# Second mixer's output projection: four couples of seven products in its middle columns, sum tiles placed elsewhere, and two couples' token sums made one chunk ahead

## The chip, the cores and the metric

The kernel runs on one core of one Trainium2 chip. The time is the device time of a whole execution in microseconds (us). The kernel before was run three times, and each comparison uses the median of its runs. One execution more was taken with the hardware profiler; all rows of a profile below come from such an execution. The engines are TensorE (PE in the profile, with PEld for its weight loads), VectorE (DVE), ScalarE (ACT), GpSimd (POOL) and SyncE (SP), which issues nearly all of the transfers from memory.

## The reference

A two-layer encoder trunk on one sequence of 256 tokens with 2048 channels, in float32. Layer 0 mixes tokens with a bidirectional mLSTM, layer 1 with a bidirectional HGRN2; after each mixer comes a ConvGLU.

```python
for layer in range(DEPTH):
    hn = rmsnorm(h, norm_mix_g[layer])
    if layer % N_MIXERS == 0:
        mix = mlstm_mixer(hn, mlstm_w_in[j], ..., mlstm_w_out[j])
    else:
        mix = hgrn_mixer(hn, hgrn_w_in[j], ..., hgrn_w_out[j])
    h = h + mix
    h = h + conv_glu(rmsnorm(h, norm_ffn_g[layer]), ...)
return rmsnorm(h, final_g)
```

The change is in the last step of each mixer, and for the second mixer alone: `y = head_rmsnorm(y, ...) * jax.nn.silu(g)` and then `y @ w_out`, a product of 256 x 2048 with 2048 x 2048 that is added to `h`.

## The kernel before

**Products.** TensorE multiplies float32 weights and activations as pairs of two rounded parts: a high part and the rest. For a weight tile `raw`, ACT makes `wh` (line 146, a copy that rounds) and DVE makes `wl = raw - wh` (line 147). Each product is three matmuls, high by high, high by low, low by high (line 235 in the stage of interest). An activation tile (`yb` in the second mixer, 128 channels by 256 tokens, high and low side by side) is made at lines 377 and 378 from a transposed head, `pz` (transposed on PE at line 1123).

**Chunks and pieces.** The program is a list of chunks. A chunk of kind "tm" makes 512 output columns, and the chunks of a projection run in the order of the list `[c0, two, c3]`: `c0` has columns 0 to 511, `two` has the middle columns 512 to 1535, `c3` the rest. Weights arrive as `raw` tiles of 128 x 2048 (1 MB, three buffers, issued on SP at line 134) and are cut into pieces of 1024 columns; the generator `split_weights` keeps the conversions three pieces ahead of their use in program order. Small jobs (`side`) are pushed as generators and advance with each product.

**The pair.** The chunk `two` is of kind "st" and is handled by `squares_by_seven`. Its unit is a couple: two blocks of 128 input channels, 16 blocks or eight couples (0 to 7) in all. A plain couple multiplies a 2 x 2 block of activations (two token halves by two channel blocks) by a 2 x 2 block of weights (two channel blocks by two groups of 512 columns) with eight products, 24 matmuls. A couple in the list `seven` does it with seven products, 21 matmuls, as in Strassen's and Winograd's scheme. For that it needs sums of weights (T1 to T4) and of tokens (S1 to S4), and four more accumulators (`mm`, beside `pc` for the four results). PE takes the pieces of a couple in this order: for a plain one first B11 and B22, then B21 and B12; for one of seven products B11 and B22, then T2 and T3, then B21 and T1, then T4.

**Where the sums come from.** Weight sums: `combine` (line 206) makes them from a raw tile when it is there, by four DVE subtractions of 128 x 512, into a tile `T` and in place in `raw`. For a stored couple, `prepare` made them in an earlier stage (line 630, in tiles `praw` of the mixer's own pool) and wrote them to a scratch in memory, `tscr`; the pair then loads `T` (line 197) and a quarter of `raw` (line 198) from there. The first mixer combines on the fly, the second has its couples 2, 4 and 6 stored. Token sums: `token` adds the two token halves of each block into a tile `f` (line 671), and `token_sums` makes four differences of 128 x 128 in it (line 565), the high part `sx` on ACT (line 566) and the low part on DVE (line 567).

**Memory and time.** The tiles `T` and `f` have two buffers each in the pool "op". In the function `mixed` that pool is opened when chunk `c0` is done, at the place of the mixer's own pool ("hg" in the second mixer), which is closed there. So the first loads and sums in "op" wait for the last readers of the old pool. `c0`'s results are added to `hm` at line 548.

**Order.** The program is written in one order, and a scheduler then sets the order in which each engine is given its instructions. The order rows below show it.

Of the kernel before, what the change touches and what calls it, by code (L numbers as in the profile page):

```python
# [8 lines left out]
F32 = mybir.dt.float32  # L9
F32R = mybir.dt.float32r  # L10
I32 = mybir.dt.int32
AF = mybir.ActivationFunctionType
ALU = mybir.AluOpType
PSUM = bass.MemoryType.PSUM

P = 128
T = 256
D = 2048
KT = D // P
# [30 lines left out]
SEVEN = (2, 3, 4, 5, 6, 7, 8, 9), (1, 2, 3, 4, 5, 6, 7)  # L50
# [1 line left out]
SPLIT = (0, 2, 5), (0, 2, 5)  # L52
END = 3
SCRATCH = 4096
SEVEN_MIX = (2, 4, 6)

QUAD = 32
TMS = (0, 4, 8, 11, 15, 18, 21)
# [6 lines left out]
def trunk_kernel(ctx, tc, xT, x_d, fg_d, pp_d, cst_d, w_gate, w_first, w_aq, w_ak, w_av, w_ao, w_aout, w_ao2,  # L65
                 w_bq, w_bv, w_bg, w_bout, w_bo2, w_up, w_d0, w_d1, w_d3, out, mscr, tscr):
    nc = tc.nc
    act, dve, pool, pe = nc.scalar, nc.vector, nc.gpsimd, nc.tensor

    keep = ctx.enter_context(tc.tile_pool(name="keep", bufs=1))  # L70
# [49 lines left out]
    side, held = Side(), []  # L120
# [61 lines left out]
    def temporary(pool_, name):  # L182
        ff = pool_.name == "ff"
        return pool_.tile([P, 1536], F32, tag="avc" if ff else name, bufs=TEMP if ff else 2, name=name)
# [207 lines left out]
    def late(dst, src):  # L392
        tc.keep_in_program_order(nc.sync.dma_start(dst, src))
# [162 lines left out]
        return where.tile([P, 2 * T], F32R, tag=f"yt{j}", name=f"{name}{j}")  # L556


    def token_sums(mp, i, a, b, S, last=None):

        m = 384 if last else 512
        sx = mp.tile([P, 2 * m], F32R, tag=f"sx{i}", name="sx")
        for i, (x, y, op) in enumerate(((a[:, P:T], b[:, P:T], ALU.add), (a[:, P:T], a[:, 0:P], ALU.subtract),
                                        (S[:, 0:P], a[:, 0:P], ALU.subtract), (b[:, 0:P], S[:, 2 * P:3 * P], ALU.subtract))):
            dve.tensor_tensor(S[:, i * P:(i + 1) * P], x, y, op)
        act.copy(sx[:, 0:m], S[:, 0:m])
        dve.tensor_tensor(sx[:, m:2 * m], S[:, 0:m], sx[:, 0:m].bitcast(F32), ALU.subtract)
        if last:
            act.copy(last[0], S[:, m:512])
            dve.tensor_tensor(last[1], S[:, m:512], last[0].bitcast(F32), ALU.subtract)  # L570
        return [(sx[:, i * P:(i + 1) * P], sx[:, m + i * P:m + (i + 1) * P]) for i in range(m // P)] + ([last] if last else [])

    def pair(src, nk, c0, x, sums, norm, seven):

        def part(t, c):
            o = 512 * (c0 + c)
            return hm[:, t, o:o + 512]

        def mid(ps):
            P1, P6, P7, P5 = ps  # L580
            u = ev.tile([P, 512], F32, tag="jk", bufs=1, name="u")
            act.copy(u, P1)
            dve.tensor_tensor(part(0, 0), part(0, 0), P1, ALU.add)
            dve.tensor_tensor(u, u, P6, ALU.add)
            dve.tensor_tensor(part(0, 1), part(0, 1), P5, ALU.add)
            dve.tensor_tensor(part(0, 1), part(0, 1), u, ALU.add)
            dve.tensor_tensor(part(1, 1), part(1, 1), P5, ALU.add)
            dve.tensor_tensor(u, u, P7, ALU.add)  # L588
            pool.tensor_tensor(part(1, 0), part(1, 0), u, ALU.add)  # L589
            pool.tensor_tensor(part(1, 1), part(1, 1), u, ALU.add)  # L590

        def done(ps):
            for c in range(2):
                for t in range(2):
                    h = part(t, c)
                    dve.tensor_tensor(h, h, ps[2 * t + c], ALU.add)
                if norm is not None and c == 0:
                    norm.add(c0)
            if norm is not None:
                side.push(second())  # L600

        def second():
            yield 3.0
            norm.add(c0 + 1)

        ch = Chunk("st", src, nk, x, done)
        ch.mid, ch.seven, ch.sums = mid, seven, sums
        ch.stored, ch.waits, ch.pool, ch.ends, ch.rest = {}, (), None, False, False
        return ch
# [29 lines left out]
    early = ([], []), ([], [])  # L639

    def prepare_early(mp, layer, first, period):
        todo, finished = early[layer]
        side.push(prepare(lambda i: [mp.tile([P, 1024], F32, tag=f"p{j}", name="praw") for j in range(2)],
                          todo, first, period, finished, late, False))

    def store(ch, src, u, todo):
        ch.stored[u] = tscr[turns["t"]]
        turns["t"] += 1
        todo.append((src[:, 2048 * u:2048 * (u + 1)], ch.stored[u]))

    def mixed(w, w2, x, norm, close, layer=None):

        c0, _, _, c3 = project(lambda c: w[c // 3], KT, x, norm)
        op, SX, first = ExitStack(), {}, c0.done

        def sums(u):
            side.until(lambda: u in SX)
            return SX[u]

        two = pair(w2, KT, 1, x, sums, norm, SEVEN_MIX)  # L660
        if layer is not None:
            for u in SEVEN_MIX:
                store(two, w2, u, early[layer][0])
            two.waits = [early[layer][1]]

        def token():
            for i, u in enumerate(SEVEN_MIX):
                f = temporary(two.pool, "f")
                for j in range(2):
                    y = x(2 * u + j).bitcast(F32)  # L670
                    dve.tensor_tensor(f[:, j * T:(j + 1) * T], y[:, 0:T], y[:, T:2 * T], ALU.add)
                SX[u] = token_sums(two.pool, i, f[:, 0:T], f[:, T:2 * T], f[:, 2 * T:4 * T])
                yield 5.0

        def done(ps):
            side.drain()
            close()
            two.pool = op.enter_context(tc.tile_pool(name="op", bufs=1))
            two.pool.tile([P, LEAD], F32, name="lead")
            first(ps)  # L680
            side.push(token())

        c0.done, c3.before = done, op.close
        return [c0, two, c3]


# [278 lines left out]
    def hgrn(norm, nxt):  # L965
        YT = [None] * KT
        stack = ExitStack()
        box = {}

        def begin():  # L970
            mp = box["mp"] = stack.enter_context(tc.tile_pool(name="hg", bufs=1))
            late(cst[:, C_LV:], cst_d[:, C_LV:])
            prepare_early(mp, 1, 30.0, 38.0)
            box["turn"] = 0
            lb = box["lb"] = mp.tile([P, KT], F32, name="lb")
            oml = box["oml"] = mp.tile([P, KT], F32, name="oml")
            t0 = mp.tile([P, 2, KT], F32, name="t0")
            t1 = mp.tile([P, KT], F32, name="t1")
            raw = pp[:, OFF["lb"]:OFF["lb"] + 2 * KT].rearrange("p (a b) -> p a b", a=2)
            dve.tensor_tensor(t1, raw[:, 0], raw[:, 1], ALU.max)  # L980
            for i in range(2):
                dve.tensor_tensor(t0[:, i], raw[:, i], t1, ALU.subtract)
            act.activation(t0, t0, AF.Exp)
            dve.tensor_tensor(t1, t0[:, 0], t0[:, 1], ALU.add)
            dve.reciprocal(t1, t1)
            for i in range(2):
                dve.tensor_tensor(t0[:, i], t0[:, i], t1, ALU.mult)
            dve.tensor_tensor(lb, t0[:, 0], t0[:, 1], ALU.add)
            dve.tensor_tensor(lb, lb, t0[:, 0], ALU.subtract)
            dve.tensor_scalar(oml, lb, -1.0, 1.0, ALU.mult, ALU.add)  # L990

        def blocks(z, h):
            return bass.AP(z.tensor, z.offset, [list(z.ap[0]), [640, 2], [2 * h, T // (2 * h)], [T + h, 2], [1, h]])
# [134 lines left out]
        chunks, vs, gs, fs = [], [], [], []  # L1128
# [26 lines left out]
        for n, ch in enumerate(fs):  # L1155
            if n in TMS:
                i = TMS.index(n)
# [4 lines left out]
        def yx(k):  # L1162
            side.until(lambda: YT[k] is not None)
            return YT[k]

        return chunks + mixed(w_bout, w_bo2, yx, nxt, stack.close, 1)


    def ffn(layer, norm, nxt):
# [91 lines left out]
    chunks = mlstm(n0, n1)  # L1261
# [3 lines left out]
    b = c[0].before  # L1265
# [85 lines left out]
def build(nc, ins, out_shape=(2, P, D), **kw):  # L1351
    ap = {k: nc.dram_tensor("in_" + k, a.shape, mybir.dt.from_np(a.dtype), kind="ExternalInput").ap()
          for k, a in ins.items()}
    out = nc.dram_tensor("out", out_shape, F32, kind="ExternalOutput").ap()
    mscr = nc.dram_tensor("mscr", (64, T), F32, kind="Internal").ap()
    tscr = nc.dram_tensor("tscr", (len(SEVEN_MIX) + 4 * len(SEVEN[0]) + 4 * len(SEVEN[1]), P, 2048), F32, kind="Internal").ap()
    with tile.TileContext(nc, schedule_with_timeline_sim=True) as tc:  # L1357
        with ExitStack() as ctx:
            trunk_kernel(ctx, tc, ap["xT"], ap["x"], ap["fg"], ap["pp"], ap["cst"], ap["w_gate"], ap["w_first"],
                         ap["w_aq"], ap["w_ak"], ap["w_av"],  # L1360
                         ap["w_ao"], ap["w_aout"], ap["w_ao2"], ap["w_bq"], ap["w_bv"], ap["w_bg"],
                         ap["w_bout"], ap["w_bo2"], ap["w_up"], ap["w_d0"], ap["w_d1"], ap["w_d3"], out, mscr, tscr, **kw)
# [12 lines left out]
```

## Time and profile before

| | |
|---|---|
| median of three runs | 2370.63 us (2369.7 to 2372.42) |
| the profiled execution | 2372.48 us, of which 2370.5 are the profile's span |
| PE busy | 2358.8 us, 14563 matmuls |
| DVE busy | 1968.9 us |
| ACT busy | 1464.2 us |
| POOL busy | 197.8 us |
| the pair of the second mixer | from about 1608 us of the span |
| TensorE's granted clock, mean | 0.999 |

A row of a timeline gives the start (us from the span's start), the length, the engine, the line, the operation, the tile written and the tiles read, their shape and type and how many such instructions follow each other; in brackets the idle time of the engine ahead of it and what ended that. On one engine the length of an instruction and the start of the next overlap a little, so the distance from start to start says what one costs. In a table of windows each engine has its busy time and, in brackets, the instructions begun.

### The profile page before, as it was taken

Reading aid. Unit: us, or ns where it says so; the run is one execution under the profiler, and the core shown is the slowest. Engines: PE = TensorE matmul, PEld = TensorE weight load, DVE = VectorE, ACT = ScalarE, POOL = GpSimd, SP = SyncE. Lnnn points to the kernel's source line nnn. Section 1 sums busy time; section 2 is a strip of 40 time slices with the busy share of each in tenths; the row PEclk is TensorE's granted clock in tenths of the full one; section 3 lists DMA queues with packets and bytes.
Section 4 is the critical chain, followed back from the end, with each engine's and each line's share of the span. In section 5 each row is a group of like instructions: output and inputs, shape, how many; then the busy total and the mean of one; then the engine's idle time right before and its main releaser. Section 6 shows DMA issues by size and latency. Waiting matters only on the chain. (4 is left out here: it accounts for less than half of the span.)

```text
span 2370.5 us, 38366 instructions
## 1 busy us (share of the span) xinstructions
PE 2358.8 (100%) x14563; PEld 2019.7 (85%) x14563; DVE 1968.9 (83%) x3033; ACT 1464.2 (62%) x2322; POOL 197.8 (8%) x244
## 2 busy tenths in 40 slices
PE   9999999999999999999999999999999999999998
PEld 8888888888888888888888888888888888888887
DVE  7777687889888898887887888778788888888888
ACT  7655456555565555665777777676555566555565
POOL 0100000000000000000232322220000000000000
PEclk9999999999999999999999999999999999999999
DMA  8776656888888888986556665546788898888896
GB/s 303 237 246 243 213 195 212 296 283 290 320 314 321 306 284 289 358 303 228 211 203 212 216 218 209 208 172 230 266 301 283 292 339 313 292 295 298 313 346 221
DMA packets 122120, 632.96 MB, mean 267 GB/s; under 512 B 13760, under 2 KB 14784, under 8 KB 77520
## 3 DMA queue, kind: packets, MB, share of 16 engines
q1 hardware_dynamic: 120240, 626.51, 74.3%
q0 software_dynamic: 1120, 3.21, 0.8%
q8 instruction: 114, 1.87, 0.3%
q10 hardware_dynamic: 576, 0.79, 0.1%
q14 instruction: 70, 0.57, 0.1%
HBM read 562.24 MB, written 68.22 MB: 266 GB/s over the span
## 5 line engine op out<-in xcount | busy, mean ns | idle before, releaser
L355 PE MATMUL mm<-xt,wh 128*128 128x512 f32 x3776 | 1312.4, 394 | 1.5 <-issue 1.5
L147 DVE TENSOR_TENSOR wl<-raw,wh 128x1024 fp32r<-128x1024 f32 (+1 forms) x844 | 1036.3, 1233 | 257.0 <-ACT wh L146 249.5
L146 ACT CAST wh<-raw 128x1024 fp32r<-128x1024 f32 (+1 forms) x844 | 876.0, 1043 | 549.2 <-PE mm L355 329.7
L359 PE MATMUL mm<-xt,wl 128*128 128x256 f32 x3776 | 1043.3, 278 | 0.0
L355 PEld LDWEIGHTS mm<-xt,wh 128*128 128x128 f32 x3776 | 705.5, 188 | 162.8 <-issue 1.8
L359 PEld LDWEIGHTS mm<-xt,wl 128*128 128x128 f32 x3776 | 709.1, 188 | 4.7
L371 PE MATMUL mm<-wh,xt 128*128 128x512 f32 x1024 | 324.4, 393 | 0.4 <-ACT wh L146 0.4
L235 PE MATMUL pc<-wh,g 128*128 128x512 f32 (+1 forms) x776 | 260.7, 388 | 0.2 <-ACT wh L146 0.2
L371 PEld LDWEIGHTS mm<-wh,xt 128*128 128x128 f32 x1024 | 191.5, 188 | 40.0 <-ACT wh L146 1.0
L630 DVE TENSOR_TENSOR praw<-praw 128x512 f32<-128x512 f32 x252 | 174.6, 693 | 32.9 <-DMA praw<-in_w_d 17.8
L371 PE MATMUL mm<-wl,xt 128*128 128x512 f32 x512 | 200.0, 391 | 0.0
L235 PEld LDWEIGHTS pc<-wh,g 128*128 128x128 f32 x776 | 145.3, 188 | 30.5 <-ACT wh L146 0.7
L235 PE MATMUL pc<-wl,g 128*128 128x512 f32 (+1 forms) x388 | 150.4, 388 | 0.0
L235 PE MATMUL mm<-wh,sx 128*128 128x512 f32 x396 | 140.5, 389 | 0.1
L147 DVE TENSOR_TENSOR wl<-T,wh 128x1024 fp32r<-128x1024 f32 (+1 forms) x132 | 126.6, 969 | 13.0 <-ACT wh L146 12.6
L146 ACT CAST wh<-T 128x1024 fp32r<-128x1024 f32 (+1 forms) x132 | 109.5, 836 | 36.5 <-DMA T<-tscr 13.4
L589 POOL TENSOR_TENSOR hm<-hm,u 128x512 f32<-128x512 f32 x10 | 14.8, 1478 | 1222.2 <-DVE u L588 1122.0
L371 PEld LDWEIGHTS mm<-wl,xt 128*128 128x128 f32 x512 | 96.2, 188 | 18.6
L1065 DVE TENSOR_TENSOR QK<-QK,G 128x256 f32<-128x256 f32 x224 | 104.7, 515 | 6.1 <-ACT kq L1044 5.7
L1189 ACT COPY avc<-mm 128x256 f32<-128x256 f32 x172 | 64.0, 373 | 72.1 <-PE mm L359 72.1
L1044 ACT COPY kq<-QK 128x512 f32<-128x512 f32 x112 | 74.5, 669 | 35.2 <-DVE QK L1065 27.6
L235 PEld LDWEIGHTS mm<-wh,sx 128*128 128x128 f32 x396 | 74.3, 188 | 15.8 <-ACT wh L146 0.5
(246 smaller groups left out, 2224.2 us busy)
## 6 DMA issues: line engine op xcount, KB each, us to landing
raw<-in_w_up SPq DMA_DIRECT2D x172, 1024.0 KB, 6.0
tscr<-praw SPq DMA_DIRECT2D x126, 512.0 KB, 6.5
praw<-in_w_d SPq DMA_DIRECT2D x120, 512.0 KB, 6.9
raw<-in_w_bq SPq DMA_DIRECT2D x48, 1024.0 KB, 4.9
T<-tscr SPq DMA_DIRECT2D x63, 768.0 KB, 8.2
raw<-in_w_d SPq DMA_DIRECT2D x60, 768.0 KB, 6.6
raw<-in_w_ao SPq DMA_DIRECT2D x24, 1024.0 KB, 4.7
raw<-in_w_d SPq DMA_DIRECT2D x24, 1024.0 KB, 7.5
```

The source lines that it names most:

```text
L146: pin(act.copy(wh[:, :m], r))
L147: pin(dve.tensor_tensor(wl[:, :m], r, wh[:, :m].bitcast(F32), ALU.subtract))
L235: pin(pe.matmul(ps, a, b, start=bank not in begun, stop=stop and i == 2))
L355: pe.matmul(ps[f], wh[:, c:c + P], x, start=k + kk == 0, stop=False)
L359: pe.matmul(ps[f][:, 0:T], wl[:, c:c + P], x[:, 0:T], start=False, stop=k + kk == ch.nk - 1)
L371: pe.matmul(ps[t], x[:, a + t * P:a + (t + 1) * P], w[:, c], start=st and i == 0, stop=sp and i == 2)
L589: pool.tensor_tensor(part(1, 0), part(1, 0), u, ALU.add)
L630: dve.tensor_tensor(out, x, y, ALU.subtract)
L1044: act.copy(m, blocks(QK, h))
L1065: dve.tensor_tensor(two[:, j], two[:, j], by[:, j], ALU.mult)
L1189: act.copy(z, p[:, T:2 * T])
```

## The change

The list of couples of seven products gets one entry for each mixer. The first mixer keeps 2, 4, 6. The second has 2, 3, 4, 6; couple 3 is not stored but combined on the fly, the other three are stored as before. The token sums of couples 2 and 3 (`AHEAD = 2`) are pushed before chunk `c0` and use the mixer's own `praw` tiles for `f` (`room`); those of 4 and 6 stay after `c0`. The results `sx` of all four couples go to tiles of the whole kernel's pool (`xt8` to `xt15`, high and low part in two tiles) and no longer to "op". In "op", two `T` tiles are allocated first, ahead of `f`.

```diff
-SEVEN_MIX = (2, 4, 6)
+SEVEN_MIX = (2, 4, 6), (2, 3, 4, 6)
+FLY_MIX = (3,)
+AHEAD = 2
...
-    def token_sums(mp, i, a, b, S, last=None):
+    def token_sums(mp, i, a, b, S, last=None, to=None):
 
         m = 384 if last else 512
-        sx = mp.tile([P, 2 * m], F32R, tag=f"sx{i}", name="sx")
+        if to is None:
+            sx = mp.tile([P, 2 * m], F32R, tag=f"sx{i}", name="sx")
+            to = sx[:, 0:m], sx[:, m:2 * m]
+        hi, lo = to
...
-        act.copy(sx[:, 0:m], S[:, 0:m])
-        dve.tensor_tensor(sx[:, m:2 * m], S[:, 0:m], sx[:, 0:m].bitcast(F32), ALU.subtract)
+        act.copy(hi, S[:, 0:m])
+        dve.tensor_tensor(lo, S[:, 0:m], hi.bitcast(F32), ALU.subtract)
...
-        two = pair(w2, KT, 1, x, sums, norm, SEVEN_MIX)
+        two = pair(w2, KT, 1, x, sums, norm, seven)
         if layer is not None:
-            for u in SEVEN_MIX:
-                store(two, w2, u, early[layer][0])
+            for u in seven:
+                if u not in FLY_MIX:
+                    store(two, w2, u, early[layer][0])
             two.waits = [early[layer][1]]
 
-        def token():
-            for i, u in enumerate(SEVEN_MIX):
-                f = temporary(two.pool, "f")
+        def token(us, step):
+            for u in us:
+                i = seven.index(u)
+                f, to = room(i) if u in seven[:ahead] else temporary(two.pool, "f"), None
+                if layer is not None:
+                    to = [keep.tile([P, 2 * T], F32R, tag=f"xt{KT // 2 + 2 * i + j}", name="sx") for j in range(2)]
                 for j in range(2):
                     y = x(2 * u + j).bitcast(F32)
                     dve.tensor_tensor(f[:, j * T:(j + 1) * T], y[:, 0:T], y[:, T:2 * T], ALU.add)
-                SX[u] = token_sums(two.pool, i, f[:, 0:T], f[:, T:2 * T], f[:, 2 * T:4 * T])
-                yield 5.0
+                SX[u] = token_sums(two.pool, i, f[:, 0:T], f[:, T:2 * T], f[:, 2 * T:4 * T], None, to)
+                yield step
...
             two.pool.tile([P, LEAD], F32, name="lead")
+            if ahead:
+                for _ in range(2):
+                    temporary(two.pool, "T")
             first(ps)
-            side.push(token())
+            side.push(token(seven[ahead:], 5.0))
...
+        if ahead:
+            c0.before = lambda: side.push(token(seven[:ahead], 10.0))
...
+        def room(i):
+            return box["mp"].tile([P, 1024], F32, tag=f"p{i % 2}", name="praw")
...
-        return chunks + mixed(w_bout, w_bo2, yx, nxt, stack.close, 1)
+        return chunks + mixed(w_bout, w_bo2, yx, nxt, stack.close, 1, room)
```

The line numbers of what follows move: 134 to 136, 146 and 147 to 148 and 149, 197 and 198 to 199 and 200, `combine` 206 to 208, `product` 235 to 237, 371 to 373, 377 and 378 to 379 and 380, 548 to 550, 565 to 567 to 570 to 572, and 671 to 681.

On DVE, at the start of the second mixer's pair, this stood in a row before. The names are those above; `yb_16676` is the last head's activation tile, and the last row's `wl` belongs to the second piece of couple 1:

```order
L671 TENSOR_TENSOR f<-yb_13286 128x256
L671 TENSOR_TENSOR f<-yb_13328 128x256
L671 TENSOR_TENSOR f<-yb_14968 128x256
L671 TENSOR_TENSOR f<-yb_15001 128x256
L565 TENSOR_TENSOR f<-f 128x128
L378 TENSOR_SCALAR yb_16676<-pz,pp,yb_16676 128x256
L565 TENSOR_TENSOR f<-f 128x128 x5
L548 TENSOR_TENSOR hm<-hm,mm 128x512
L565 TENSOR_TENSOR f<-f 128x128
L548 TENSOR_TENSOR hm<-hm,mm 128x512
L565 TENSOR_TENSOR f<-f 128x128
L147 TENSOR_TENSOR wl<-raw,wh 128x1024
```

The four sums at the top are those of couples 2 and 4. With the change DVE has at that place, to begin with:

```order
L681 TENSOR_TENSOR f<-yb_14970 128x256
L681 TENSOR_TENSOR f<-yb_15003 128x256
L208 TENSOR_TENSOR T<-raw 128x512
L681 TENSOR_TENSOR f<-yb_16518 128x256
L681 TENSOR_TENSOR f<-yb_16624 128x256
L570 TENSOR_TENSOR f<-f 128x128
L380 TENSOR_SCALAR yb_16689<-pz,pp,yb_16689 128x256
L570 TENSOR_TENSOR f<-f 128x128
L208 TENSOR_TENSOR raw<-raw 128x512
L570 TENSOR_TENSOR f<-f 128x128 x3
```

The sums are those of couples 4 and 6, and two of couple 3's combinations (line 208) have come between. DVE goes on with:

```order
L550 TENSOR_TENSOR hm<-hm,mm 128x512 x2
L208 TENSOR_TENSOR T<-raw 128x512
L570 TENSOR_TENSOR f<-f 128x128 x2
L149 TENSOR_TENSOR wl<-T,wh 128x1024
L149 TENSOR_TENSOR wl<-raw,wh 128x1024
L208 TENSOR_TENSOR T<-raw,T 128x512
L570 TENSOR_TENSOR f<-f 128x128
L149 TENSOR_TENSOR wl<-raw,wh 128x1024 x3
```

The first of the three at the end is the second piece of couple 1, the last row of the order before. All four combinations now stand ahead of it, and so do `wl<-T` of couple 2 and the first piece of couple 3, which stood behind it.

On PE, in couple 1 of the same pair, the order before was as follows; `yb_11555` is an activation tile of couple 0, `yb_12367` and `yb_12063` are those of couple 1's two blocks:

```order
L235 MATMUL pc<-wh,yb_11555 128x512
L235 MATMUL pc<-wh,yb_12367 128x512
L235 MATMUL pc<-wh,yb_12063 128x512
L235 MATMUL pc<-wh,yb_12367 128x512
L235 MATMUL pc<-wh,yb_12063 128x512
L235 MATMUL pc<-wl,yb_12367 128x512
L235 MATMUL pc<-wh,yb_12367 128x512
L235 MATMUL pc<-wl,yb_12063 128x512
```

Four matmuls with `wh` stood between the end of the couple ahead and the first with `wl`. With the change there are:

```order
L237 MATMUL pc<-wh,yb_12369 128x512
L237 MATMUL pc<-wh,yb_12065 128x512
L237 MATMUL pc<-wh,yb_12369 128x512
L237 MATMUL pc<-wh,yb_12065 128x512
L237 MATMUL mm<-wh,yb_13288 128x512
L237 MATMUL mm<-wh,sx 128x512 x2
L237 MATMUL mm<-wl,sx 128x512
L237 MATMUL mm<-wh,sx 128x512
L237 MATMUL mm<-wl,sx 128x512
L237 MATMUL mm<-wh,sx 128x512 x2
L237 MATMUL pc<-wl,yb_12369 128x512
```

Eight matmuls of couple 2 (those into `mm`) have moved ahead of couple 1's first with `wl`.

On ACT, `wh` of couple 1's second piece stood ahead of `wh<-T` of couple 2 and of couple 3's first piece, and now stands behind the two. On SP, the load of `T` for couple 4 stood right behind that for couple 2, and now stands behind the raw loads of couples 4 and 5. Over the whole program PE has three matmuls fewer in the pair.

More of the change, by code (lines that the diff above doesn't have):

```diff
@@ L570, in token_sums @@
             dve.tensor_tensor(last[1], S[:, m:512], last[0].bitcast(F32), ALU.subtract)
-        return [(sx[:, i * P:(i + 1) * P], sx[:, m + i * P:m + (i + 1) * P]) for i in range(m // P)] + ([last] if last else [])
+        return [(hi[:, i * P:(i + 1) * P], lo[:, i * P:(i + 1) * P]) for i in range(m // P)] + ([last] if last else [])
     def pair(src, nk, c0, x, sums, norm, seven):
@@ L649, in store, with mixed @@
         todo.append((src[:, 2048 * u:2048 * (u + 1)], ch.stored[u]))
-    def mixed(w, w2, x, norm, close, layer=None):
+    def mixed(w, w2, x, norm, close, layer=None, room=None):
         c0, _, _, c3 = project(lambda c: w[c // 3], KT, x, norm)
         op, SX, first = ExitStack(), {}, c0.done
+        seven, ahead = (SEVEN_MIX[0], 0) if layer is None else (SEVEN_MIX[1], AHEAD)
         def sums(u):
@@ L972, in begin @@
             late(cst[:, C_LV:], cst_d[:, C_LV:])
+            for j in range(2):
+                room(j)
             prepare_early(mp, 1, 30.0, 38.0)
@@ L1355, in build @@
     mscr = nc.dram_tensor("mscr", (64, T), F32, kind="Internal").ap()
-    tscr = nc.dram_tensor("tscr", (len(SEVEN_MIX) + 4 * len(SEVEN[0]) + 4 * len(SEVEN[1]), P, 2048), F32, kind="Internal").ap()
+    tscr = nc.dram_tensor("tscr", (len(SEVEN_MIX[1]) + 4 * len(SEVEN[0]) + 4 * len(SEVEN[1]), P, 2048), F32, kind="Internal").ap()
     with tile.TileContext(nc, schedule_with_timeline_sim=True) as tc:
```

## Prediction

> **What bounds the kernel now.** I read the page's list of engines first, then TensorE's waits over the whole span, then the stage that the change touches.
>
> ```profile
> span 2370.5 us, 38366 instructions
> PE 2358.8 (100%) x14563; PEld 2019.7 (85%) x14563; DVE 1968.9 (83%) x3033; ACT 1464.2 (62%) x2322; POOL 197.8 (8%) x244
> ```
>
> ```profile
> PE mm L355 <- issue: 1.5, 1, 1.5
> PE idle L1258 <- POOL ones L1251: 1.1, 1, 1.1
> PE mm L371 <- ACT wh L146: 0.4, 1, 0.4
> PE pc L235 <- DVE wl L147: 0.3, 1, 0.3
> ```
>
> TensorE (PE) is the bound: it is busy for the span, and its named waits (total, times, longest) come to 3.3 us in these four rows, the largest there are. So an edit can gain only the matmuls that it takes away and the few tenths that PE stands still, but it can lose whatever it makes PE wait. The pair of the second mixer holds one of those waits, the last row. Its place, with the busy time of each engine (PE, PEld, DVE, ACT, POOL, then the granted clock, DMA share, GB/s):
>
> ```profile
> 1605.00:1610.00 5.00, 5.00 (x24) 3.94 (x22) 5.00 (x16) 1.82 (x3) 0.00 (x0) 1.00 0.78 280
> 1610.00:1615.00 5.00, 4.65 (x21) 3.55 (x20) 5.00 (x6) 5.00 (x8) 0.00 (x0) 1.00 0.69 242
> ```
>
> VectorE (DVE) has no free time for ten microseconds here, at the very start of the pair, and that is where the change adds work to it. PE's timeline at the wait (start, length, instruction, idle before it):
>
> ```profile
> 1608.99 1.37 PE L235 MATMUL pc<-wh,yb 128*128 128x512 f32 x5
> 1610.71 0.50 PE L235 MATMUL pc<-wl,yb 128*128 128x512 f32 x1 [0.35 <-DVE wl L147]
> 1611.05 0.39 PE L235 MATMUL pc<-wh,yb 128*128 128x512 f32 x1
> 1611.28 0.39 PE L235 MATMUL pc<-wl,yb 128*128 128x512 f32 x1
> ```
>
> Successive starts give 0.23 us a matmul (1611.05 to 1611.28; 0.227 over longer stretches). Five from 1608.99 are through at 1610.13, and the sixth starts at 1610.71: a stall of 0.58 us, in which PE needs the low half (wl) of couple 1's second piece. DVE comes to that late:
>
> ```profile
> 1604.85 1.43 DVE L671 TENSOR_TENSOR f<-yb 128x256 f32<-128x256 f32 x4 [2.94 <-PE pz L1123]
> 1606.20 0.29 DVE L565 TENSOR_TENSOR f<-f 128x128 f32<-128x128 f32 x1
> 1606.40 0.48 DVE L378 SCALAR_TENSOR_TENSOR yb<-pz,pp,yb 128x256 fp32r<-128x256 f32 x1
> 1606.80 1.09 DVE L565 TENSOR_TENSOR f<-f 128x128 f32<-128x128 f32 x5
> 1607.84 0.69 DVE L548 TENSOR_TENSOR hm<-hm,mm 128x512 f32<-128x512 f32 x1
> 1608.44 0.29 DVE L565 TENSOR_TENSOR f<-f 128x128 f32<-128x128 f32 x1
> ...
> 1609.44 1.22 DVE L147 TENSOR_TENSOR wl<-raw,wh 128x1024 fp32r<-128x1024 f32 x1
> 1610.65 1.23 DVE L147 TENSOR_TENSOR wl<-T,wh 128x1024 fp32r<-128x1024 f32 x1
> 1611.79 2.35 DVE L147 TENSOR_TENSOR wl<-raw,wh 128x1024 fp32r<-128x1024 f32 x2
> ```
>
> From 1604.85, when PE's last transposes release it, DVE goes without a gap, and the row that PE waits for is the seventeenth.
>
> **The change, part by part.** All sums are against this profiled execution (2372.48 us, 2.0 of it outside the span); the runs' median is 2370.63, so I add the net to the median.
>
> Matmuls: a fourth couple does 21 matmuls in place of 24. Gain 3 x 0.227 = 0.68 us, all on PE's path. If the old stall of 0.58 us went too, the gain would be 1.26; that is the best end.
>
> The combinations of couple 3, which nothing prepares early, are four subtractions of 128x512 on DVE. The first mixer's pair makes its combinations in the same way:
>
> ```profile
> 331.65 0.69 DVE L206 TENSOR_TENSOR T<-raw 128x512 f32<-128x512 f32 x1
> 332.25 1.22 DVE L147 TENSOR_TENSOR wl<-raw,wh 128x1024 fp32r<-128x1024 f32 x1
> ```
>
> One takes 0.60 us from start to start, so the four take 2.40. In the changed order all four stand ahead of the low half that PE already waits for. So do two conversions, of couple 2's T and of couple 3's first piece, which came behind it before. I add up the rows that now stand ahead of couple 1's second wl, from the same release at 1604.85: four f sums 1.35 (1604.85 to 1606.20), four combinations 2.40, eight small f<-f 1.60 (0.20 each, 1606.20 to 1606.40), the yb row 0.40, two hm rows 1.20 (0.60 each, 1607.84 to 1608.44), wl<-T 1.14 (1610.65 to 1611.79), wl of couple 3's first piece 1.14. That is 9.23, so it starts at 1614.08. The same sum without combinations and conversions gives 4.55, that is 1609.40, and the trace has 1609.44, so the way of adding holds. From that row's start to the matmul it releases went 1610.71 - 1609.44 = 1.27, so PE can go on at 1615.35.
>
> ScalarE (ACT) makes the high halves (wh) and puts couple 1's second piece third now, where it was first:
>
> ```profile
> 1608.06 1.06 ACT L146 CAST wh<-raw 128x1024 fp32r<-128x1024 f32 x1 [2.73 <-PE mm L371]
> 1609.57 1.05 ACT L146 CAST wh<-T 128x1024 fp32r<-128x1024 f32 x1 [0.45 <-DVE f L565]
> 1610.52 2.00 ACT L146 CAST wh<-raw 128x1024 fp32r<-128x1024 f32 x2
> ```
>
> With wh<-T at 1609.57 as before, the second of the two that follow, now couple 1's, ends at 1612.52. PE needs it for four matmuls from 1609.22 on, so PE's wait begins there: up to 3.3 us. After it stand 12 matmuls (these four and eight of couple 2, which the order has moved ahead of the wl ones): 1612.52 + 12 x 0.227 = 1615.24. ACT's chain and DVE's end within 0.1 us of each other, so neither alone being faster would help.
>
> The price: undisturbed, the first wl matmul would start after 13 matmuls from 1608.99, at 1611.94. It starts at 1615.35, 3.41 late. The eight moved matmuls are not done again later, so of this 0.58 was there before: 2.83 more. Net 2.83 - 0.68 = **2.15 us slower**.
>
> What could make DVE's chain start earlier is the memory: a T tile's load and the first f wait for the transposes, because their memory is that of the closing pool.
>
> ```profile
> SPq L197 <- PE pz L1123: 6.4, 1, 6.4
> ...
> 1604.90 0.80 SPq L197 DMA_DIRECT2D T<-tscr  x2
> 1610.69 0.33 SPq L134 DMA_DIRECT2D raw<-in_w_bo  x1
> ```
>
> The changed order still has TensorE among the waits of both, so I take 1604.90 and 1604.85. Otherwise only the rows ahead of the yb row (four f, one combination, one f<-f: 1.35 + 0.60 + 0.20 = 2.15) could run before the release, since the yb row itself needs the transposes' result; the loss then falls by up to 2.15, to nothing.
>
> The early token sums of couples 2 and 3: four f rows (1.35), eight f<-f (1.60), two low parts (0.60 each, as for the 128x512 rows above) are 4.15 us of DVE; with two ACT copies they go up to 90 us ahead of the pair, into windows such as this one:
>
> ```profile
> 1570.00:1580.00 10.00, 10.00 (x49) 8.35 (x49) 8.79 (x21) 9.39 (x21) 0.00 (x0) 1.00 0.34 117
> ```
>
> PE is full in it and DVE has 1.2 us free in the ten, so the sums fill the free time of some 35 us, and they have about 90. I take nothing; without cover it could cost up to 4.15. What it relieves is the pair's sums: rows of two couples still stand at the start (4, 6 now, 2, 4 before), so the 9.23 is not shortened.
>
> SP issues the same number of loads, but raw of couple 4 is free only when couple 1's low half is done: from 1610.69 to about 1615.3. The load of T for couple 4 went as the second at 1605.28 and now waits for a T buffer: after 1614.08 come three conversions (3.42) and four rows of 0.60, so about 1620.
>
> ```profile
> 1620.00:1625.00 5.00, 5.00 (x24) 4.14 (x23) 4.31 (x7) 1.83 (x4) 0.00 (x0) 1.00 0.98 333
> ```
>
> ```profile
> DMA to landing us min/median/max: 4.6/6.1/6.4
> ...
> T<-tscr SPq DMA_DIRECT2D x63, 768.0 KB, 8.2
> ```
>
> The first row is T's landing time in this stage, the second the kernel's median. PE comes to couple 4's raw 48 matmuls after 1615.35, at 1626.2, and to its T after 62, at 1629.4. Landing after 6.4 plus a 1.05 cast gives 1622.8 and 1627.5: 1.9 us to spare for T. I take nothing; both ends stand in the second rival.
>
> **The rivals.**
>
> No new wait, or a shorter one. For it: the first mixer makes three couples' combinations on the fly, and PE does not stop there.
>
> ```profile
> 320.00:325.00 5.00, 5.00 (x24) 4.14 (x23) 5.00 (x10) 2.49 (x3) 0.00 (x0) 1.00 0.56 210
> ```
>
> Against it: here the trace has DVE held back by 2.94 us just before the pair. If T's memory is free early, the net is 2.15 - 2.15 = 0, 2370.6; if no wait is left at all, -1.26, 2369.4.
>
> Late transfers of couple 4, the rival on the slow side. The place is T's matmuls at 1629.4, the price is what its landing has over 8.3 us (1629.4 - 1620.0 - 1.05), and it makes the kernel slower than 2375.4 from a landing of about 10.9 on; at 12 it is 2.15 + 3.7 = 5.8, 2376.5. For it: the kernel's median of 8.2, and queues at 0.98 share in 1620 to 1625. Against it: 6.4 is the most in this stage, and at 333 GB/s the three loads in flight then (about 2.3 MB) take 7 us.
>
> A slower clock after the wait. A gap of 1.5 us left the granted clock at full:
>
> ```profile
> 1224.00:1228.00 4.00, 2.54 (x15) 1.98 (x14) 2.34 (x8) 2.94 (x8) 0.58 (x1) 1.00 0.79 317
> 5.41 1.64 PE L371 MATMUL mm<-wh,xt 128*128 128x512 f32 x4
> 6.88 0.63 PE L371 MATMUL mm<-wl,xt 128*128 128x512 f32 x2
> ```
>
> At the program's start, though, four matmuls took 1.47 us (5.41 to 6.88), 0.14 more each than later. If a wait of 3.3 brought that back, it would cost 0.56 for four, and 3.4 for 15 at twice the spacing: 2373.3 to 2376.2. The Trainium skill ("TensorE: Matmul & The Clock Gate", section "HAM oscillation — how this bites in real kernels") has TensorE fall back to half clock when it idles through a window of about 3.4 us. By that rule a gap of 3.3 just misses the bound; the 1.5 us gap agrees with it, and no run here shows one long enough to test it.
>
> **How the numbers follow.** Forecast 2370.63 + 2.15 = 2372.8, chance 0.62. No or a shorter wait (2369.4 to 2370.6): 0.16. Late transfers (2375.4 to 2376.5): 0.14. Slower clock (half of it beyond 2375.4): 0.05. The remaining 0.03 is for something unseen, either way. The measurement tells about 0.2% from no change, 4.7 us: faster means below 2365.9, which only the unseen reaches, 0.02; slower means above 2375.4, 0.14 + 0.02 = 0.16; the same 0.82. The range goes from 2370.2, within the first rival, to 2375.4, where the late transfers begin.
>
> **What would show it.** Right: in PE's waits a row at the pair's start, wh or wl at line 237, of some 3 us together; DVE full from 1604.85 to about 1620 with the four L208 rows inside; T of couple 4 issued about 1620; PE's count down by about 3 (some records may be missing); the granted clock 1.00 in that stage. Wrong: DVE's first f well before PE's transposes; a wait under 1 us at that place; a PE wait on a DMA of T or raw at couple 4; PE waits of their own near the early sums.

## The result, and the profile after

The changed kernel took 2378.85 us in the median of seven runs (2376.26 to 2383.62), the kernel before 2370.20 in seven runs beside them (2369.6 to 2372.42). The ratio is 1.0035, with a 95% interval of 1.0025 to 1.0045: 8.65 us slower, where 2.15 were forecast. The profiled execution is the slowest of the seven: it took 2383.62 us, 11.1 more than that of before. Most of that has to be found outside the forecast.

The page of the changed kernel begins:

```profile
span 2381.7 us, 38378 instructions
PE 2365.1 (99%) x14560; PEld 2023.4 (85%) x14560; DVE 1972.8 (83%) x3046; ACT 1465.6 (62%) x2325; POOL 197.0 (8%) x244
```

TensorE has three matmuls fewer and is busy for 6.3 us more. Its waits (total, times, longest):

```profile
PE pc L237 <- ACT wh L148: 2.8, 1, 2.8
PE mm L357 <- issue: 2.3, 1, 2.3
PE mm L373 <- ACT wh L148: 1.7, 2, 1.1
...
PE pc L237 <- DVE wl L149: 0.3, 1, 0.3
```

The first row is new and is the wait at the pair's start that the prediction names. The timeline of PE there:

```profile
1612.67 0.39 PE L237 MATMUL pc<-wh,yb 128*128 128x512 f32 x1
1615.84 2.07 PE L237 MATMUL pc<-wh,yb 128*128 128x512 f32 x4 [2.79 <-ACT wh L148]
1617.71 0.63 PE L237 MATMUL mm<-wh,yb 128*128 128x512 f32 x1
1618.14 0.98 PE L237 MATMUL mm<-wh,sx 128*128 128x512 f32 x2
1618.95 0.39 PE L237 MATMUL mm<-wl,sx 128*128 128x512 f32 x1
```

and the windows around it, with the granted clock as the third figure from the end:

```profile
1610.00:1615.00 5.00, 3.06 (x13) 1.90 (x11) 5.00 (x14) 2.15 (x3) 0.00 (x0) 1.00 0.34 133
1615.00:1620.00 5.00, 4.16 (x12) 3.36 (x13) 5.00 (x7) 4.44 (x8) 0.00 (x0) 0.66 0.11 15
```

Behind the wait the clock is granted at 0.66 in the mean of five microseconds, that is half clock for 3.4 of them ((1 - 0.66) x 5 / 0.5). The four matmuls from 1615.84 come 0.47 apart (1.87 to the next start), twice the usual 0.227. From 1612.67 to the first matmul with couple 1's wl, at 1620.09, PE does 13 matmuls; at 0.227 they need 2.95, so 4.5 us are lost, of which about 1.5 belong to the half clock (seven matmuls in 3.1 us from 1615.84 to 1618.95 in place of 1.6). Less the old 0.58 and the 0.68 for three matmuls, the pair's start costs 3.2 us net in this execution.

That leaves 8 us elsewhere. Two equal windows in the first up projection of layer 1's ConvGLU, of before and then of after:

```profile
1750.00:1800.00 50.00, 50.00 (x291) 43.75 (x290) 44.36 (x74) 28.51 (x46) 0.00 (x0) 1.00 0.84 303
```

```profile
1750.00:1800.00 50.00, 50.00 (x285) 43.35 (x284) 43.38 (x75) 27.77 (x45) 0.00 (x0) 1.00 0.85 292
```

PE is full in both, at full clock, and does 285 matmuls in place of 291. Nothing waits; each matmul takes longer. The timeline of the changed kernel shows where that sets in, at an exchange of two neighbouring matmuls which both kernels make in the second chunk of that projection. It is the place where two matmuls of 512 columns and then two of 256 follow each other (the rows with x2):

```profile
1687.01 0.39 PE L357 MATMUL mm<-xt,wh 128*128 128x512 f32 x1
1687.24 0.28 PE L361 MATMUL mm<-xt,wl 128*128 128x256 f32 x1
1687.35 0.39 PE L357 MATMUL mm<-xt,wh 128*128 128x512 f32 x1
...
1689.44 0.62 PE L357 MATMUL mm<-xt,wh 128*128 128x512 f32 x2
1689.91 0.40 PE L361 MATMUL mm<-xt,wl 128*128 128x256 f32 x2
...
1691.91 0.40 PE L357 MATMUL mm<-xt,wh 128*128 128x512 f32 x1
1692.15 0.28 PE L361 MATMUL mm<-xt,wl 128*128 128x256 f32 x1
1692.26 0.40 PE L357 MATMUL mm<-xt,wh 128*128 128x512 f32 x1
1692.49 0.28 PE L361 MATMUL mm<-xt,wl 128*128 128x256 f32 x1
1692.61 0.40 PE L357 MATMUL mm<-xt,wh 128*128 128x512 f32 x1
1692.85 0.28 PE L361 MATMUL mm<-xt,wl 128*128 128x256 f32 x1
1692.97 0.40 PE L357 MATMUL mm<-xt,wh 128*128 128x512 f32 x1
```

Ahead of the exchange two matmuls take 0.347 us together (0.34 to 0.35 from start to start), behind it 0.353 (three pairs in 1.06 from 1691.91 to 1692.97), and so to the end of the projection at about 1925. Over 234 us that is 234 x (1 - 0.347/0.353) = 4 to 4.4 us. In the kernel before it is the other way round: 0.353 ahead of the exchange, 0.347 behind it. From its first matmul to its last the projection takes 245.45 us before (1669.16 to 1914.61) and 249.81 after (1675.88 to 1925.69): 4.36 us more.

A third place is the gap of 2.3 us "issue" above, at 1226, which is 1.5 us long in the profile of before; here half clock follows it too:

```profile
1225.00:1230.00 5.00, 2.73 (x15) 2.20 (x14) 3.31 (x9) 3.66 (x10) 0.00 (x0) 0.98 0.62 226
1230.00:1235.00 5.00, 5.00 (x21) 4.16 (x21) 3.17 (x8) 2.88 (x8) 0.00 (x0) 0.68 0.36 87
```

That is 0.8 of a longer gap and about 1.6 of half clock, 2.4 us, in a stage that the change does not touch. A fourth is a wait on a wl of DVE at 1984.6, the 0.3 us row among the waits above. The four make 3.2 + 4.4 + 2.4 + 0.3 = 10.3 of the 11.1 us.

### The profile page after: what moved, and what is told of

It reads as the page before. It is cut to its first block, busy times and chain, and to the rows that moved or that the text cites. A ratio compares the mean times of both kernels' runs of the same rounds, so it can differ in the third digit from the quotient of the medians.

```text
span 2381.7 us, 38378 instructions
## 1 busy us (share of the span) xinstructions
PE 2365.1 (99%) x14560; PEld 2023.4 (85%) x14560; DVE 1972.8 (83%) x3046; ACT 1465.6 (62%) x2325; POOL 197.0 (8%) x244
## 3 DMA queue, kind: packets, MB, share of 16 engines
q8 instruction: 114, 1.87, 0.3%
```

## The experiments

| run | median, us | over the kernel before, run beside it | ratio, 95% interval |
|---|---|---|---|
| e1_again | 2378.59 | +6.85 | 1.0020 to 1.0042 |
| e2_fly6 | 2370.92 | -0.82 | 0.9993 to 1.0010 |
| e3_three | 2372.31 | +0.57 | 0.9992 to 1.0010 |
| e4_store | 2378.86 | +7.12 | 1.0021 to 1.0044 |
| e5_after_noswap | 2375.89 | +4.70 | 1.0010 to 1.0027 |
| e6_before_noswap | 2376.34 | +5.15 | 1.0012 to 1.0030 |
| e7_fly6_sums3 | 2371.63 | +0.44 | 0.9992 to 1.0009 |
| e8_longer_wait | 2379.58 | +8.39 | 1.0019 to 1.0042 |
| e9_fly6_turn | 2370.19 | -1.23 | 0.9987 to 1.0005 |
| e10_after_two_undone | 2374.04 | +2.62 | 1.0002 to 1.0020 |
| e11_after_turn | 2379.21 | +7.52 | 1.0022 to 1.0047 |
| e12_fly6_turn_again | 2371.36 | -0.33 | 0.9990 to 1.0008 |

The kernel before had medians of 2371.74 (beside e1 to e4), 2371.19 (e5 to e8), 2371.42 (e9 and e10) and 2371.69 (e11 and e12), with single runs from 2368.4 to 2375.1.

**The changed kernel again (e1_again), no edit.**

> The changed kernel once more, nothing edited. Its first profile was 11.2 us longer than the profile of before, in three places: about 2.4 us at 1226 (an issue gap of 2.3 us, and the half clock behind it), about 3.8 net at the pair's start (a 2.8 us wait and 3.4 us of half clock behind it), and about 5 in the first up stage of layer 1's ConvGLU, where two matmuls take 0.353 us together and not 0.347. Theory: only the pair's part belongs to the change; the other two fall differently from execution to execution. Then this profile has the 2.8 us wait again, but the steps of 0.353 or the half clock at 1226 need not be there, and its runs spread over 2374 to 2384. Rival: all three are fixed by the program; then this profile shows all three, and its span is again about 2381.

All seven runs lay between 2377.67 and 2379.78. The profile (span 2376.6) has the wait again, 2.5 us, and the 0.353 us step again, but neither the gap at 1226 nor half clock behind the pair's wait:

```profile
1610.00:1615.00 5.00, 3.47 (x14) 2.39 (x15) 5.00 (x8) 5.00 (x10) 0.00 (x0) 1.00 0.00 0
1615.00:1620.00 5.00, 5.00 (x23) 4.13 (x22) 5.00 (x7) 3.25 (x6) 0.00 (x0) 1.00 0.88 275
```

So the wait and the long step came back together, against the theory's half that took the step for chance; the gap at 1226 and the half clock are what differs from execution to execution.

**Another couple on the fly (e2_fly6).** `FLY_MIX = (3,)` becomes:

```diff
-FLY_MIX = (3,)
+FLY_MIX = (6,)
```

> As the changed kernel (four couples, two couples' sums early, sums in x tiles, T first), but couple 3 is stored and couple 6 is combined on the fly, so the four subtractions come about 20 us later and couple 1's second piece stands first again on DVE and ACT. Theory (the order at the pair's start makes the loss): the 2.8 us wait is gone, only the old wait of about 0.6 us is left, no half clock behind it, and the time is 2369 to 2370 but for chance steps elsewhere. Rival (the sums' place in memory or the early sums make it): the time stays at 2374 or more.

The four subtractions, the four couples, the early sums and the places in memory are those of the changed kernel; only the couple that is combined on the fly is later, and couple 3 is stored in place of 6. The wait of 2.8 is gone, the old one is back, and one is left in layer 1:

```profile
PE pc L237 <- DVE wl L149: 1.1, 2, 0.8
```

```profile
1970.85 0.50 PE L237 MATMUL pc<-wl,g 128*128 128x512 f32 x1 [0.76 <-DVE wl L149]
```

The time cannot be told from that of the kernel before; 2370.92 lies a little above the 2369 to 2370 of the theory and far from the rival. What made the pair's start slow is where couple 3's combinations stand and the order that comes with them, not a fourth couple, the early sums or the memory. The step in layer 1 is 0.347 us here.

**Three couples (e3_three).**

```diff
-SEVEN_MIX = (2, 4, 6), (2, 3, 4, 6)
-FLY_MIX = (3,)
+SEVEN_MIX = (2, 4, 6), (2, 4, 6)
+FLY_MIX = ()
```

> As the changed kernel, but with the three couples 2, 4, 6 of the kernel before, all stored: what is left of the change is the early sums of couples 2 and 4, the sums in x tiles and the T tiles first. Theory (order of couple 3's combinations): 2370 to 2371, a wait of about 0.8 us at the pair's start. Rival (memory and early sums cost): above 2374, with PE waits between 1510 and 1600 or at the pair's start.

Not to be told from before either (2372.31 is above the 2370 to 2371 forecast, beside a kernel before of 2371.74); the pair's wait on DVE's wl is 0.6 us. The early sums and the x tiles cost nothing that shows; the interval would leave room for about 2 us.

**Couple 3 stored (e4_store).**

```diff
-FLY_MIX = (3,)
+FLY_MIX = ()
```

> As the changed kernel, but couple 3 is prepared early and loaded like the others: no subtraction on DVE at the pair's start, one load of T and of a quarter of raw more. Theory: the 2.8 us wait shrinks to about 1 us; but four couples prepared early need more of DVE before the pair (four more subtractions and two stores), and T of couple 3 comes by a transfer, so some 1.5 us of waits may stand between 1600 and 1610; 2370.5 to 2372. Rival (a fourth couple of seven products costs by itself, by its loads): above 2374.

A miss: 7.1 us over before, and the rival's bound of 2374 is passed. PE's waits around the pair are these:

```profile
1602.32 0.50 PE L373 MATMUL mm<-wh,yb 128*128 128x512 f32 x1 [0.67 <-ACT yb L379]
1604.65 0.30 PE L1143 MATMUL pz<-cst,y 128*128 128x128 f32 x1 [0.59 <-DVE y L1137]
1615.29 0.50 PE L237 MATMUL pc<-wl,yb 128*128 128x512 f32 x1 [0.67 <-DVE wl L149]
```

The last, at the pair's start, is as short as forecast, but ahead of the pair more is lost than forecast. From about 1555 to the pair's first matmul this profile falls 2.6 us back behind that of before; about 1.5 were forecast for waits there. The largest part is the long step, which this kernel has too (285 matmuls in 1750 to 1800; 249.85 us for the projection, 4.4 more than before), without any long wait at the pair. So the long step does not need that wait.

**The exchange left out, in the changed kernel (e5_after_noswap) and in the kernel before (e6_before_noswap).** In both, one line, by which two neighbouring matmuls of the second up chunk of layer 1 stand in the usual order:

```diff
-  swap=(2,) if part and i == 0 else (3,) if f0 + i == 1 else (), paced=True))
+  swap=(2,) if part and i == 0 else (3,) if f0 + i == 1 and layer == 0 else (), paced=True))
```

> The changed kernel, with one thing else: in layer 1 the second chunk of the ConvGLU's up projection no longer exchanges two neighbouring matmuls (swap at 3), which both kernels do. Nothing else moves on any engine. In all traces so far the step of two matmuls in that stage changes at this exchange: in the kernel before from 0.353 to 0.347 us, in the changed kernel from 0.348 to 0.353, and it stays so to the stage's end. Theory (the exchange turns over whichever of two rhythms TensorE is in, and the change had turned it once more ahead of it): without it the changed kernel stays at 0.347 and gains about 4.7 us, to 2373.5 to 2374.5. Rival (the slow step belongs to the changed kernel's memory or loads): still 0.353, 2378 or more.

> The kernel before with the same exchange of two matmuls left out in layer 1. Theory (turning over): it stays in the slow rhythm it has ahead of the exchange, 0.353 us through the first up stage of layer 1, and loses about 4.7 us, to 2375 to 2377, though nothing of the change is in it. Rival: no difference, 2370 to 2372.

The window 1750 to 1800 of the first, and then of the second:

```profile
1750.00:1800.00 50.00, 50.00 (x290) 43.71 (x290) 44.37 (x77) 29.16 (x49) 0.00 (x0) 1.00 0.84 294
```

```profile
1750.00:1800.00 50.00, 50.00 (x285) 43.36 (x284) 43.90 (x74) 28.31 (x47) 0.00 (x0) 1.00 0.84 296
```

The step turned over in both: the kernel before, with nothing of the change in it, does 285 matmuls and is 5.15 us slower than with the exchange; the changed kernel does 290. In time the changed kernel gained 2.15 us against before (6.85 to 4.70) and not 4.7; its profile has half clock behind the pair's wait and the gap at 1226, which that of e1_again had not, so part of the gain may be hidden by these. The projection itself took 245.37 us in e5 and 249.91 in e6. Between e11 and e10, which also differ by the exchange alone, it is 4.90.

**Three couples' sums ahead (e7_fly6_sums3).** As e2, with:

```diff
-AHEAD = 2
+AHEAD = 3
```

> As the kernel with couple 6 on the fly, with the token sums of three couples (2, 3, 4) made ahead in place of two: two f sums and four differences less on DVE at the pair's start. Theory (DVE's row of work from the release to couple 1's second wl sets the wait): that row gets 0.68 + 0.80 us shorter but for one sum's low half (0.60) that moves ahead, so the old wait of 0.58 shrinks or stays; 2369 to 2371. Rival (early sums cost where they are put): over 2372.

No gain: the wait at the pair's start is 0.5 and that in layer 1 1.1 us. DVE comes to couple 1's second wl 4.78 us after its release (1603.63 to 1608.41), against 4.59 in e2 (1602.47 to 1607.06). The sum's low half, 0.60, stands in that row, and ahead of line 550 DVE stands still for 0.77 us until PE has `c0`'s results, so the row does not get shorter with fewer sums in it.

**A longer wait (e8_longer_wait).** The four combinations and couple 1's second piece are kept in program order:

```diff
-                dve.tensor_tensor(out, x, y, ALU.subtract)
+                pin(dve.tensor_tensor(out, x, y, ALU.subtract))
...
-                yield *parts(r[:, 1024:2048], 1024, more=ch.pool), 1
+                yield *parts(r[:, 1024:2048], 1024, more=ch.pool, **keep_), 1
```

(`keep_` passes the same `pin` for couple 1 of this pair.)

> The changed kernel with couple 3's four combinations and couple 1's second piece kept in program order among themselves. That gives an order in which couple 1's second piece comes later still: behind couple 2's T, couple 3's first piece, two low sums and two combinations. Theory (what PE waits for is this piece, by the sum of the rows ahead of it): one wait of about 5 us at the pair's start, about 2 more than in the changed kernel, and, since it is longer than 3.4 us, half clock behind it in every execution; 2379 to 2383 with the slow rhythm. Rival (other things set the loss): the time of the changed kernel, 2378 to 2379.

```profile
1616.21 2.08 PE L237 MATMUL pc<-wh,yb 128*128 128x512 f32 x4 [5.44 <-ACT wh L148]
```

```profile
1610.00:1615.00 5.00, 0.77 (x4) 0.31 (x2) 3.88 (x7) 4.04 (x7) 0.00 (x0) 0.82 0.01 5
1615.00:1620.00 5.00, 3.79 (x9) 3.05 (x10) 5.00 (x7) 3.05 (x5) 0.00 (x0) 0.50 0.17 34
```

One wait of 5.4 us, as forecast, with half clock for 6.8 us (0.18 x 5 / 0.5 in the first window, all of the second). The forecast of the long step was wrong: this kernel has 0.347. So the loss of 8.4 us is made here without it, for the most part of the wait with the half clock (6.1 us more than before from the pair's first matmul to the up projection, 74.48 in place of 68.37) and of a wait of 1.2 us in layer 1. That the time, 2379.58, lies inside the 2379 to 2383 of the theory is luck, since the long step was counted in there.

**The shifted buffers (e9_fly6_turn, e10_after_two_undone, e11_after_turn, e12_fly6_turn_again).** A piece's tiles come from one of two pools by a running count, every third from the pair's own. Two pieces more shift that count for all that follows, and with it the order of 342 matmuls of layer 1's later stages. The edit, in e9 and e12 on e2, in e11 on the changed kernel, in e10 on e5:

```diff
+        if len(ch.seven) == 4 and ch.nk == KT:
+            turns["w"] += 1
```

> As the kernel with couple 6 on the fly, and behind the pair the count of pieces, by which every third piece goes to the stage's own pool, is moved on by one. A fourth couple adds two pieces and so shifts that count for all that follows; moved on by one, each engine's order in layer 1's ConvGLU is that of the kernel before again. Theory (the shift is the third part of the loss: in the kernels with four couples PE stands still for 0.4 to 1.3 us at about 1970 to 1980, in layer 1's first pair, for a wl of DVE, and not in those with three): that wait goes, and what is left is the kernel before less 0.68; 2369.5 to 2370.5, about 0.8 below the kernel with couple 6 on the fly. Rival (the wait belongs to something else): 2371, as before.

> The changed kernel, couple 3 on the fly at the pair's start, with the other two losses undone: no exchange in layer 1's second up chunk (fast rhythm), and the count of pieces moved on by one (order of layer 1's ConvGLU as before). Theory (three parts that add up: the pair's wait, the rhythm, the shifted buffers): what is left is the pair's start alone, the wait of 2.6 to 2.8 with what follows it, less the old 0.58 and 0.68: about 2 us over the kernel before, and 1.7 more in executions where half clock follows: 2373 to 2375. Rival (the parts do not add up): 2376 or more, or no difference from before.

> The changed kernel with one thing else: the count of pieces moved on by one behind the pair, so that layer 1's ConvGLU has the order of the kernel before again; the exchange of two matmuls is there, so the slow rhythm should be too. Theory (parts add up): about 1 to 1.5 us below the changed kernel, 2377 to 2377.5, with the wait at 1970 to 1980 gone and 0.353 us steps in layer 1's first up stage. Rival: the shifted buffers also set the rhythm; then 0.347 and about 2373.

> The kernel with couple 6 on the fly and the count of pieces moved on, once more, to see how far it lies below the kernel before. Theory: 0.7 to 1.2 us below, 2369.5 to 2370.5, with the fast rhythm again and no wait but the old one at the pair's start. Rival (chance made the first result): the kernel before's time within 0.3 us.

With it TensorE's order in layer 1 is that of the kernel before, and the waits at 1970 to 1985 are gone from all four profiles. The time does not show this surely: e9 is 0.4 us lower than e2 against before, e12 0.5 higher (0.33 us below before, nearer to its rival, within 0.3 us, than to its theory, 0.7 to 1.2 below), e11 0.7 higher than e1_again (a miss of its forecast by 2 us; its step is 0.353, so the buffers do not set that). e10, with the exchange left out as well, is 2.62 us over before, inside its forecast. So the best version found, four couples with couple 6 on the fly, has 1.2 and 0.3 us less than before in two measurements, and both intervals hold 1: it was not shown to beat the kernel before. In e12's profile the step lengthens in the middle of the stage, from 290 matmuls in a window of 50 us to 285:

```profile
1750.00:1800.00 50.00, 50.00 (x290) 43.73 (x289) 40.17 (x67) 26.26 (x42) 0.00 (x0) 1.00 0.79 281
1850.00:1900.00 50.00, 50.00 (x285) 43.38 (x284) 42.87 (x72) 29.07 (x48) 0.00 (x0) 1.00 0.83 293
```

## Why the prediction was wrong, by its own steps

**What bounds the kernel: right.** No gain showed in any version beyond what three matmuls and the old stall could give.

**DVE's row of work: right in length.** Forecast were 9.23 us from the release by PE's transposes to the start of couple 1's second wl. The timeline of DVE in the changed kernel, with its first and last rows:

```profile
1608.26 0.76 DVE L681 TENSOR_TENSOR f<-yb 128x256 f32<-128x256 f32 x2 [2.94 <-PE pz L1143]
1608.94 0.68 DVE L208 TENSOR_TENSOR T<-raw 128x512 f32<-128x512 f32 x1
...
1617.49 3.49 DVE L149 TENSOR_TENSOR wl<-raw,wh 128x1024 fp32r<-128x1024 f32 x3
```

1617.49 - 1608.26 = 9.23. In e1 it is 9.23 too (1604.14 to 1613.37), and PE goes on with that wl at 1614.65, 1.28 later, where 1.27 was forecast. (The row that PE waited for before is the sixteenth from the release, not the seventeenth; and the pair's first matmul before stands at 1600.79, not at about 1608.) The release is as late as before, so the first rival (memory free early, no new wait) has fallen: the T load still went out behind the transposes. ACT's three conversions also came one after another, and PE's wait was named wh, of 2.5 to 2.8 us in five profiles where up to 3.3 was forecast. ACT in the changed kernel:

```profile
1612.85 1.04 ACT L148 CAST wh<-T 128x1024 fp32r<-128x1024 f32 x1 [4.12 <-DMA T<-tscr]
1613.80 3.88 ACT L148 CAST wh<-raw 128x1024 fp32r<-128x1024 f32 x4
```

It stood idle for 4.12 us until couple 2's T had landed, with couple 1's second piece behind that in its order (the second of the four). In e2 that piece is ACT's first again, at 1605.68, ahead of the T at 1607.07. So it is the order on ACT, as much as the four subtractions on DVE, that makes the wait.

**The price at the pair: right in size.** From the pair's first matmul to the first of the up projection e1, which has no half clock there, takes 70.50 us (1600.08 to 1670.58) and the kernel before 68.37 (1600.79 to 1669.16): 2.13 more, where 2.15 were forecast. e10, which undoes what was lost elsewhere, is 2.62 us over before (interval 0.5 to 4.7).

**The slower clock: the rival came true, at a chance of 0.05.** Half clock for 3.4 us followed the pair's wait in the first profile, in e5, e10 and e11, and 6.8 us of it in e8; not in e1. It costs 1.5 us of slower matmuls, 1.0 to 1.35 net (71.50 to 71.85 us from the pair's first matmul to the up projection in those four, against 70.50 in e1), between the 0.56 and the 3.4 that the prediction gave as ends. The error was to weigh it by the length of the gap forecast. The Trainium skill ("TensorE: Matmul & The Clock Gate", section "Part 1: The HAM clock gate (the "warmup" mystery)") has the clock fall after an idle window of about 3.4 us, and a window that runs freely. The 3.4 us of half clock agree with the window's length; that it needs so long a gap does not: 2.3 us at 1226 and 2.5 to 2.8 at the pair were enough. Gaps of 1.5 to 2.0 us at 1226 in other profiles were not.

The traces also show why e1 was spared. In each of them the granted clock changes only at points of a grid of 3.413 us, which lies differently in every execution. In the changed kernel it falls to 0.5 at 1229.77 and at 1615.48, 113 steps apart, and is back one step later. In the 14 traces, the program's first and last microseconds left out, half clock followed every step of the grid of which TensorE stood still for 2.09 us or more (seven steps, the least in e5) and none of which it stood still for 1.89 us or less. The 1.89 is e1's: a point of the grid, at 1610.86, lies within its gap (1608.97 to 1611.45) and splits it into 1.89 and 0.59. So the same wait brings half clock or not by where it falls on the grid. What counts between 1.89 and 2.09 no trace shows.

**Late transfers of couple 4: this rival did not come.** The load of T went out at 1624.16, 15.9 after the release (forecast about 15.2), and no profile shows PE waiting for a DMA there.

**The step that failed is the sum's end at the pair.** The sum 2370.63 + 2.15 holds no term for what comes behind the pair's start, and the range had only couple 4 for that; no rival went beyond 2376.5, so 2378.85 was left to the 0.03 for something unseen. The largest part, 4 to 5 us, is there: the step of the matmuls in layer 1's up projection, 0.353 in place of 0.347. e6 shows that this needs nothing of the change, only one exchange of two matmuls fewer; e5, e10 and e11 that undoing the exchange or keeping it moves the changed kernel by the same step. The prediction priced neither that step nor the new order of layer 1's rows. The half clock, put at nothing in the sum, is the next part. The shifted buffers are a smaller part: waits of 0.3 to 1.2 us in the profiles, within the scatter in time.

**What stays open.** Why the changed kernel comes to the exchange with the short step and the kernel before with the long one. The step turns short 6.2 us into the projection in the changed kernel, e1, e5, e10 and e11 alike, at 9.4 in e4, and not ahead of the second chunk in the others; the order of PE is the same up to there, and the rows of DVE and ACT agree within 0.02 us. It goes with the program (five of five profiles of couple 3 on the fly in the scheduler's own order), but e8 has the same work and does not have it. No run told what in it sets the step.

## What to carry to other kernels

When TensorE is the bound, an edit is worth what it does to the row of work ahead of the piece that TensorE needs next: add up that row from its release, as here, before adding work to it, and put added work behind the piece, as with couple 6 in place of 3. Price the stages behind the edit too: count a buffer rotation on past the edited stage, and compare the step of equal matmuls there in both profiles, since a full engine can be slower with no wait at all. A single wait of two to three microseconds on TensorE should be priced with half clock behind it as one of two outcomes: here it followed five of six such gaps.

## What the runs showed of the hardware that was not expected

In layer 1's first up projection TensorE ran the same stream of matmuls in two steady rhythms, with full clock and no wait: 0.347 and 0.353 us for one of 512 and one of 256 columns, 1.9% apart. One exchange of two neighbouring matmuls turned the one into the other, in both directions, and it held for over 200 us; in one execution (e12) it turned in the middle of the stage with no cause that the profile shows.

Half clock came after gaps of 2.3 to 2.8 us and lasted 3.4 us, and 6.8 after one of 5.4; after 2.5 us in e1 it did not come. It began and ended at points of a grid of 3.413 us, behind each step that was idle for 2.09 us or more, and behind none that was idle for 1.89 or less. The same program's gap at 1226 was 2.3 us in one execution and not there in another.
